# One gate block earlier beside the read-back of y, and a two-part order for two input blocks of layer 1

## The chip, the cores and the metric

The kernel runs on one core of one Trainium2 chip. The time is that of the device in microseconds (us); of several runs the median is given. PE is the matrix engine, DVE the vector engine, ACT the activation engine, POOL the general engine, and SP the queue that issues nearly all DMAs.

## What is computed

One inference step of a two-layer (`DEPTH = 2`) hybrid backbone over 1152 tokens, 128 of context and 1024 latent, with 1024 channels. Cut to what matters:

```python
h = rmsnorm(x, norm_g) * (1.0 + scale) + shift
a_in, a_gate, f_in, f_gate, q, k, v, c_gate = jnp.split(h @ w_in, SPLITS, axis=-1)
ya, finals = s5_mixer(a_in, ...)                    # the state-space branch; its result is "y"
za = jax.nn.gelu(ya) @ glu_w
ya = za[..., :BRANCH_W] * jax.nn.sigmoid(za[..., BRANCH_W:])
yf = fourier_mix(f_in) @ fnet_w
yc = blocked_attention(rope(q), rope(k) + context, v + context)
proj = [branch_n * silu(gate_n) @ w_branch[n] for n in (a, f, c)]
g = jax.nn.sigmoid(h @ merge_w + merge_b)           # three gates of 1024 channels
out = x + gate * (sum(g[n] * proj[n]) @ w_out)
```

## The kernel before

**Dense blocks.** Nearly all PE work is in dense blocks: 128 output channels for the 1152 tokens. The tokens are three chunks (j = 0, 1, 2) of 384. A value is held as a rounded high part and a low part, and each product is three matmuls (high x high, low x high, high x low): a block over 1024 channels is 3 x 8 x 3 = 72 matmuls of 128x384, one over 512 channels is 36. Results go to a PSUM tile `pd`, of which there are two; ACT or DVE empties it ("evicts") before the next but one chunk can start. Weights are loaded by SP into `wst` (512 rows at a time), split by ACT (`whi`) and POOL (`wlo`) one unit ahead; a chunk's inputs are `hh`/`hl` for h, and the tile `A1` (rows show it as A) for a branch's values read back from DRAM.

**A list and its driver.** `layer` fills a list of blocks in a fixed order with `dense_add`, and `dense(n)` takes the next n from it. It yields after each 4 input groups, so a gate block has 6 steps of 12 matmuls and a block over 512 channels has 3. `drive`, `beside` and `run_some` mix these steps with other work. The framework's scheduler then orders each engine's instructions by its own forecast, so that work may move ahead of the place where it was written. Every engine runs its instructions in that order and waits at the first that can't run.

**Stages that matter here, in each layer.** (1) Input blocks: `a_in` first (`store_blocks`, 4 blocks), while the last chunk of h is still being normalised at the start of layer 1 (`h_gen(l + 1, xT, acc, (2,))`). (2) Scan and output of the state-space branch, which ends with y in DRAM. (3) The "u" stage: y is read back and split (`zload_landed`: 12 loads `yl`, then a number of bare yields, then 12 splits on ACT and DVE into A1), beside gate blocks; then 8 Glu blocks, with the modulation sums of `ada_side_gen` (`aacc`, DVE) beside them. (4) The "f" stage: the Fourier branch, beside 4 gate blocks. (5) The "a" stage: attention. It is 64 steps (8 heads x 8 groups of 128 queries). A step is: 6 matmuls of scores (`pa`), their maximum on DVE (`at_mx`), exp on ACT (`at_P`), scaling on DVE, 9 transposes on PE, their split on ACT and DVE (`at_PT`); every second step ends with 18 matmuls (`pv`). There is one `pa`, so the next scores wait for the exp. Each step hands one dense step to PE: `run_some(m, k)`. Over the stage attention yields room for 78 dense steps, and `merges` holds 18 + 6 + 24 + 6 + 24 = 78. (6) The "c" stage: the attention's result is read back and split (`zload_gen(zc_d, ...)`), beside gate blocks whose results `thc` live in a pool that opens when attention's pool closes.

Of the kernel before, what the change touches and what calls it, by code (L numbers as in the profile page):

```python
# [11 lines left out]
AF = mybir.ActivationFunctionType  # L12
# [19 lines left out]
C_AIN, C_AG, C_FIN, C_FG, C_Q, C_KV, C_CG = 0, 512, 1024, 1536, 2048, 2560, 2816  # L32
# [70 lines left out]
class Program:  # L103
# [1186 lines left out]
    def zload_landed(self, z_d, zf, tag):  # L1290
        ts = []
        for j in range(3):
            for b in range(4):
                t = self.sb(tag, [128, 384], bufs=12, pool=self.gp)
                self.dma_rows(z_d, b, j, t, False)
                ts.append((j, b, t))
        for _ in range(3):
            yield 1
        for i, (j, b, t) in enumerate(ts):
            s = slice(384 * j, 384 * j + 384)  # L1300
            self.act(zf[:, 0, b, s], t)
            self.tt(zf[:, 1, b, s], t, zf[:, 0, b, s].bitcast(F), OP.subtract)
            if i % 4 == 3:
                yield 1
# [29 lines left out]
    def layer(self, l, cs):  # L1334
        nc, I = self.nc, self.I
        w_in = I["w_in"][l]
        dt_ = lambda n, shape, ty=F: self.dp.tile(list(shape), ty, name=f"{n}{l}")
        f_d, za_d, zb_d, zc_d = (dt_(n, (512, NT)) for n in ("fd", "zad", "zbd", "zcd"))
        a_d, y_d = ((dt_(n + "p", (512, SP)), dt_(n + "l", (512, SL))) for n in ("ad", "yd"))
# [10 lines left out]
        zt = {}  # L1350

        def rows(d, b, j):
            return d[128 * b:128 * b + 128, 384 * j:384 * j + 384]

        def th_tile(tag="th", bufs=3):
            return self.sb(tag, [128, 384], bufs=bufs, pool=self.gp)

        def glu_blocks():
            out = []
            for b in range(4):  # L1360
                th = {}
                def evb(j, ps, th=th):
                    th[j] = th_tile()
                    self.act(th[j], ps, AF.Tanh, scale=0.5)
                def eva(j, ps, b=b, th=th):
                    sg = self.jt(rows(sg_d[0], b, j))
                    o = self.jo()
                    self.stt(o, th.pop(j), 1.0, ps, OP.add, OP.mult)
                    self.stt(o, o, 0.5, sg, OP.mult, OP.mult)
                    self.dma(rows(za_d, b, j), o)  # L1370
                r = zrhs(lambda: zt["y"])
                out.append(dict(w=self.colblk(I["glu_w"][l], 512, b, 4), nk=4, rhs=r, evac=evb))
                out.append(dict(w=self.colblk(I["glu_w"][l], 0, b, 4), nk=4, rhs=r, evac=eva))
            return out
# [15 lines left out]
        def gate_block(n, b, th):  # L1390
            def ev(j, ps):
                t = self.jo() if "d" in th else th_tile("thc", 24) if n == 2 else th_tile()
                self.act(t, ps, AF.Tanh, bias=self.hmb[l][:, 8 * n + b:8 * n + b + 1], scale=0.5)
                if "d" in th:
                    self.dma(rows(th["d"], b, j), t)
                else:
                    th[j] = t
            return dict(w=self.colblk(I["merge_w"][l], 1024 * n, b), nk=8, rhs=self.rhs_h, evac=ev)
# [22 lines left out]
        thb = {"d": dt_("thb", (D, NT))}  # L1421
# [30 lines left out]
                                rhs=lambda k, j: (self.mh[j][:, k], self.ml[j][:, k]), evac=ev))  # L1452
            return out

        self.dense_add(self.store_blocks(w_in, C_AIN, 4, a_d, AF.Copy))
        self.dense_add(self.store_blocks(w_in, C_FIN, 4, f_d, AF.Copy))
        self.dense_add(self.store_blocks(w_in, C_AG, 4, sg_d[0], AF.Silu))
        self.dense_add(self.store_blocks(w_in, C_FG, 4, sg_d[1], AF.Silu))
        self.dense_add(self.store_blocks(w_in, C_CG, 4, sg_d[2], AF.Silu))
        self.dense_add([gate_block(0, b, tha) for b in range(8)])  # L1460
        self.dense_add([gate_block(1, 0, thb)])
        self.dense_add(glu_blocks())
        self.dense_add([gate_block(1, b, thb) for b in range(1, 6)])
        self.dense_add(fw_blocks())
        self.dense_add([gate_block(1, 6, thb)])
        self.dense_add([proj_block(0, b, tha, "a") for b in range(8)])
# [7 lines left out]
        run = self.run_all  # L1474
        with self.spool:
            with self.epool:
                if l == 0:
                    with self.pool("gp", l, "s"):
                        drive((self.dense(4), 40), (self.ssm_setup_gen(l), 2))
                else:  # L1480
                    run(self.dense(4))
                if l == 0:
                    for k in range(KD):
                        self.dma(self.xT_d[0][128 * k:128 * k + 128, :], self.xT0[:, k])
                with self.pool("gp", l, "m"):
                    drive((self.dense(4), 47), (self.state_gen(l, a_d), 29))
            with self.pool("qp", l):
                with self.pool("gp", l, "q"):
                    self.qkt = self.qkv_tables(l)
                    def qkv():  # L1490
                        yield from self.qkv_gen(l, qs_d, k_d, v_d, (0,))
                        yield from self.qkv_gen(l, qs_d, k_d, v_d, (1,))
                    q = qkv()
                    self.run_some(q, 8)
                    drive((self.scan_gen(l), 103), (self.dense(12), 140))
                    drive((q, 78), (self.dense(2), 21))
                    self.finals(l)
                with self.pool("gp", l, "o"):
                    drive((self.dense(6), 12*6), (self.ssm_out_gen(l, a_d, y_d), 33), (self.qtail_gen(), QT))
        with self.pool("gp", l, "u"):  # L1500
            zt["y"] = self.sb("A1", [128, 2, 4, NT], R)
            run(self.beside(self.zload_landed(y_d, zt["y"], "yl"), self.dense(1), 1))
            drive((self.dense(8), 47), (self.ada_side_gen(l, self.gp, (4, 5)), 6))
        with self.pool("gp", l, "f"):
            self.fnet_tables()
# [2 lines left out]
            drive((self.dense(3), 48), (self.fnet_gen(l, f_d, zt["f"]), 48))  # L1508
        with self.pool("gp", l, "a"):
            def merges():  # L1510
                yield from self.dense(5)
                zt["a"] = self.sb("A1", [128, 2, 4, NT], R)
                yield from self.beside(self.zload_gen(za_d, zt["a"], False, HELD), self.dense(1), NA)
                yield from self.dense(8)
                zt["b"] = self.sb("A1", [128, 2, 4, NT], R)
                yield from self.beside(self.zload_gen(zb_d, zt["b"], False, 2), self.dense(1), 1)
                yield from self.dense(8)
            m = merges()
            for k in self.attn_gen(l, qs_d, k_d, v_d, sg_d[2], zc_d):
                self.run_some(m, k)  # L1520
            run(m)
# [65 lines left out]
    def run(self):  # L1587
        self.open_ssm(0)
        with ExitStack() as cs:
            self.np_ = cs.enter_context(self.tc.tile_pool(name="np", bufs=1))  # L1590
            self.xp = cs.enter_context(self.tc.tile_pool(name="xp", bufs=1))
            self.setup()
            self.xT0 = xT = self.sb("A1", [128, KD, NT])
            ssq = self.sb("ssqt", [128, 2, 9], pool=self.xp)
            self.rb = {}
            self.xr0 = self.sb("xr0", [128, KD, 384], pool=self.xp)
            ada = self.ada_first_gen(0, self.xp, (2, 0, 3, 1))
            xg = self.x_gen(xT, ssq)
            self.run_some(xg, 6)
            self.h_tiles((0,))  # L1600
            self.rb_first(ssq, 0)
            for k in range(KD):
                self.xr_first(xT, k)
            next(ada)
            self.run_some(xg, 2)
            next(ada)
            self.run_some(xg, 4)
            self.h_tiles((1,))
            self.rb_first(ssq, 1)
            for k in range(4):  # L1610
                self.h_first(xT, 0, k)
            next(ada)
            for k in range(2):
                self.h_first(xT, 1, k)
            next(ada)
            with self.tc.high_priority():
                for k in range(4, 8):
                    self.h_first(xT, 0, k)
            self.run_all(ada)
            for k in range(2, 5):  # L1620
                self.h_first(xT, 1, k)
            self.run_all(xg)
            self.h_tiles((2,))
            self.rb_first(ssq, 2)
            for k in range(5, 8):
                self.h_first(xT, 1, k)
            for k in range(KD):
                self.h_first(xT, 2, k)
        for l in range(DEPTH):
            for j in range(3):  # L1630
                self.debug(f"hh{l}", self.hh[j].bitcast(F), (slice(None), slice(None), slice(384 * j, 384 * j + 384)))
            with ExitStack() as cs:
                xT, acc = self.layer(l, cs)
                if l + 1 < DEPTH:
                    self.run_all(self.h_gen(l + 1, xT, acc, (2,)))
                else:
                    self.run_all(self.final_gen(xT, acc, (2,)))
# [25 lines left out]
```

## Time and profile before

| what | us |
|---|---|
| median of 3 runs | 2710.02 (2704.8 to 2712.21) |
| the profiled execution | 2707.93 |
| its span, first to last instruction | 2706.2 |
| PE busy in the span | 2599.8 |
| DVE, ACT, POOL busy | 1746.8, 1200.5, 655.4 |

The times are of the whole launch; the span leaves out 1.7 us around the first and the last instruction. The start of a matmul in the trace is measured and its end modelled, so a full stream of 128x384 matmuls shows rows that overlap.

### The profile page before, as it was taken

To read this page: it belongs to the slowest core of one execution; us is meant where nothing else is said; L and a number is where in the kernel's file an instruction comes from. 1 tells how busy PE (TensorE), PEld (TensorE's weight loads), DVE (VectorE), ACT (ScalarE), POOL (GpSimd) and SP (SyncE) were. 2 spreads that over 40 slices of the span, in tenths; PEclk is the share of its full clock that TensorE was granted. 3 is DMA by queue.
4 is the path that set the end of the run, shared out by engine and by line. 5 is a ranking of instruction groups with operands and counts; after the bars stand their busy time and mean duration, and the time that the engine had idled before them with its cause. 6 is when DMAs were issued, how large, how long until landed. Compare 5 with 4: busy or idle time off the path is not lost. (4 is left out here: it accounts for less than half of the span.)

```text
span 2706.2 us, 44496 instructions
## 1 busy us (share of the span) xinstructions
PE 2599.8 (96%) x16093; PEld 2502.1 (92%) x16093; DVE 1746.8 (65%) x3837; ACT 1200.5 (44%) x2754; POOL 655.4 (24%) x518
## 2 busy tenths in 40 slices
PE   6999999999999999999999999989999999999998
PEld 4999999899999899999989999989999998999997
DVE  6559964636478889847462798564654788981443
ACT  5462245741355465423345322575224556543244
POOL 1332122312321020132333312232222212101223
PEclk8999999999999999999999999999999999999999
DMA  7533233566443435535542322345645334442334
GB/s 258 154 103 102 90 105 106 168 185 199 149 139 110 143 118 154 188 96 138 172 134 86 112 86 83 119 131 166 210 142 192 104 116 155 148 125 80 92 117 145
DMA packets 459812, 366.85 MB, mean 136 GB/s; under 512 B 72816, under 2 KB 431816, under 8 KB 459592
## 3 DMA queue, kind: packets, MB, share of 16 engines
q1 hardware_dynamic: 458168, 359.68, 43.4%
q0 software_dynamic: 1424, 4.33, 0.5%
q8 instruction: 127, 2.08, 0.3%
q14 instruction: 93, 0.76, 0.1%
HBM read 243.52 MB, written 120.39 MB: 134 GB/s over the span
## 5 line engine op out<-in xcount | busy, mean ns | idle before, releaser
L169 PE MATMUL pd<-hh,whi 128*128 128x384 f32 x2496 | 854.3, 343 | 8.8 <-ACT jo L143 4.5
L169 PE MATMUL pd<-hh,wlo 128*128 128x384 f32 x2496 | 842.9, 338 | 4.7 <-POOL wlo L146 4.4
L169 PE MATMUL pd<-hl,whi 128*128 128x384 f32 x2496 | 840.2, 337 | 0.8 <-DVE hl L150 0.8
L146 POOL TENSOR_TENSOR wlo<-wst,whi 128x512 fp32r<-128x512 f32 x312 | 432.8, 1389 | 1523.1 <-ACT whi L143 1445.4
L169 PEld LDWEIGHTS pd<-hh,whi 128*128 128x128 f32 x2496 | 470.9, 189 | 14.9 <-ACT jo L143 6.1
L169 PEld LDWEIGHTS pd<-hh,wlo 128*128 128x128 f32 x2496 | 470.8, 189 | 10.0 <-POOL wlo L146 9.0
L169 PEld LDWEIGHTS pd<-hl,whi 128*128 128x128 f32 x2496 | 471.3, 189 | 2.9 <-DVE hl L150 1.9
L169 PE MATMUL pd<-A,whi 128*128 128x384 f32 x1728 | 457.7, 341 | 6.3 <-ACT jo L143 6.3
L143 ACT ACTIVATE whi<-wst 128x512 fp32r<-128x512 f32 x312 | 195.6, 630 | 291.1 <-PE pd L169 188.2
L169 PEld LDWEIGHTS pd<-A,whi 128*128 128x128 f32 x1728 | 310.9, 189 | 9.0 <-ACT jo L143 6.9
L169 PE MATMUL pd<-A,wlo 128*128 128x384 f32 x864 | 293.5, 340 | 0.0
L1107 DVE TENSOR_REDUCE at_mx<-pa 128x1 f32<-128x1152 f32 x128 | 173.2, 1353 | 16.0 <-PE pa L169 15.6
L143 ACT ACTIVATE at_PT<-pt 128x384 fp32r<-128x384 f32 (+1 forms) x260 | 114.9, 490 | 142.6 <-PE pt L174 142.2
L169 PE MATMUL pa<-at_K,at_Q 128*128 128x384 f32 x768 | 167.1, 347 | 7.8 <-ACT at_P L143 5.3
L143 ACT ACTIVATE at_P<-pa,at_mx 128x1152 f32<-128x1152 f32 x128 | 158.0, 1235 | 20.6 <-DVE at_mx L1107 19.4
L169 PEld LDWEIGHTS pd<-A,wlo 128*128 128x128 f32 x864 | 163.2, 189 | 0.1
L169 PEld LDWEIGHTS pa<-at_K,at_Q 128*128 128x128 f32 x768 | 128.2, 188 | 28.2 <-ACT at_P L143 25.2
L169 PE MATMUL pt<-qkW,hh 128*128 128x384 f32 x576 | 151.9, 345 | 0.5 <-DVE qk_xn L146 0.5
L169 PE MATMUL pv<-at_PT,at_V 128*128 128x256 f32 x1152 | 148.8, 283 | 0.0
L143 ACT ACTIVATE jo<-pd 128x384 f32<-128x384 f32 x120 | 58.1, 485 | 199.9 <-PE pd L169 113.0
L169 PEld LDWEIGHTS pv<-at_PT,at_V 128*128 128x128 f32 x1152 | 144.7, 191 | 0.8
L146 DVE TENSOR_TENSOR at_PT<-pt,at_PT 128x384 fp32r<-128x384 f32 (+1 forms) x260 | 133.1, 550 | 9.3 <-ACT at_PT L143 8.6
(297 smaller groups left out, 3719.5 us busy)
## 6 DMA issues: line engine op xcount, KB each, us to landing
aw<-in_ada_w_dram SPq DMA_DIRECT2D x48, 512.0 KB, 4.5
wst<-in_merge_w_dram SPq DMA_DIRECT2D x96, 256.0 KB, 2.9
wst<-in_w_in_dram SPq DMA_DIRECT2D x80, 256.0 KB, 3.0
td<-jo SPq DMA_DIRECT2D x96, 192.0 KB, 1.9
jt<-td SPq DMA_DIRECT2D x96, 192.0 KB, 2.7
wst<-in_w_out_dram SPq DMA_DIRECT2D x64, 256.0 KB, 2.8
sgd<-jo SPq DMA_DIRECT2D x72, 192.0 KB, 1.8
jt<-sgd SPq DMA_DIRECT2D x64, 192.0 KB, 3.0
```

The lines of the kernel that those rows point to most:

```text
L143: return self.nc.scalar.activation(out, in_, func, **kw)
L146: return (e or self.nc.vector).tensor_tensor(out=out, in0=a, in1=b, op=op)
L169: return self.nc.tensor.matmul(out, w, x, start=first, stop=last, **kw)
L1107: nc.vector.tensor_reduce(out=mx[:, 0:1], in_=src, axis=AX.XY if m3 else AX.X, op=OP.max, negate=True)
```

## The change

In the u stage of both layers two gate blocks stand beside the read-back of y instead of one, and the splits start after five bare yields instead of three. The second gate block comes out of the attention stage, whose `merges` starts with `dense(4)` instead of `dense(5)`: the Fourier stage still takes four gate blocks, each one further on in the list. Attention then has room for 78 dense steps, and `merges` holds 72. In layer 1 alone, the first two of the four `a_in` blocks are cut in two parts: chunks 0 and 1 of both, then chunk 2 of both. Each part loads and splits its weights, so four weight units more are loaded, and `dense(6)` covers the same twelve chunks as `dense(4)` did.

```diff
--- before.py
+++ after.py
@@ -1294,7 +1294,7 @@
                 t = self.sb(tag, [128, 384], bufs=12, pool=self.gp)
                 self.dma_rows(z_d, b, j, t, False)
                 ts.append((j, b, t))
-        for _ in range(3):
+        for _ in range(5):
             yield 1
         for i, (j, b, t) in enumerate(ts):
             s = slice(384 * j, 384 * j + 384)
@@ -1452,15 +1452,18 @@
                                 rhs=lambda k, j: (self.mh[j][:, k], self.ml[j][:, k]), evac=ev))
             return out
 
-        self.dense_add(self.store_blocks(w_in, C_AIN, 4, a_d, AF.Copy))
+        ain = self.store_blocks(w_in, C_AIN, 4, a_d, AF.Copy)
+        if l > 0:
+            ain = [dict(ain[b], js=js) for js in ((0, 1), (2,)) for b in (0, 1)] + ain[2:]
+        self.dense_add(ain)
         self.dense_add(self.store_blocks(w_in, C_FIN, 4, f_d, AF.Copy))
         self.dense_add(self.store_blocks(w_in, C_AG, 4, sg_d[0], AF.Silu))
         self.dense_add(self.store_blocks(w_in, C_FG, 4, sg_d[1], AF.Silu))
         self.dense_add(self.store_blocks(w_in, C_CG, 4, sg_d[2], AF.Silu))
         self.dense_add([gate_block(0, b, tha) for b in range(8)])
-        self.dense_add([gate_block(1, 0, thb)])
+        self.dense_add([gate_block(1, b, thb) for b in (0, 1)])
         self.dense_add(glu_blocks())
-        self.dense_add([gate_block(1, b, thb) for b in range(1, 6)])
+        self.dense_add([gate_block(1, b, thb) for b in range(2, 6)])
         self.dense_add(fw_blocks())
         self.dense_add([gate_block(1, 6, thb)])
         self.dense_add([proj_block(0, b, tha, "a") for b in range(8)])
@@ -1478,7 +1481,7 @@
                     with self.pool("gp", l, "s"):
                         drive((self.dense(4), 40), (self.ssm_setup_gen(l), 2))
                 else:
-                    run(self.dense(4))
+                    run(self.dense(6))
                 if l == 0:
                     for k in range(KD):
                         self.dma(self.xT_d[0][128 * k:128 * k + 128, :], self.xT0[:, k])
@@ -1499,7 +1502,7 @@
                     drive((self.dense(6), 12*6), (self.ssm_out_gen(l, a_d, y_d), 33), (self.qtail_gen(), QT))
         with self.pool("gp", l, "u"):
             zt["y"] = self.sb("A1", [128, 2, 4, NT], R)
-            run(self.beside(self.zload_landed(y_d, zt["y"], "yl"), self.dense(1), 1))
+            run(self.beside(self.zload_landed(y_d, zt["y"], "yl"), self.dense(2), 1))
             drive((self.dense(8), 47), (self.ada_side_gen(l, self.gp, (4, 5)), 6))
         with self.pool("gp", l, "f"):
             self.fnet_tables()
@@ -1508,7 +1511,7 @@
             drive((self.dense(3), 48), (self.fnet_gen(l, f_d, zt["f"]), 48))
         with self.pool("gp", l, "a"):
             def merges():
-                yield from self.dense(5)
+                yield from self.dense(4)
                 zt["a"] = self.sb("A1", [128, 2, 4, NT], R)
                 yield from self.beside(self.zload_gen(za_d, zt["a"], False, HELD), self.dense(1), NA)
                 yield from self.dense(8)
```

The first place is ACT's order in the u stage of layer 0: `jo<-pd` is the eviction of a gate chunk, `A_6450<-yl` a split of y, `th<-pd` the eviction of a Glu chunk. Before:

```order
L143 ACTIVATE A_6450<-yl 128x384 x3
L143 ACTIVATE whi<-wst 128x512
L143 ACTIVATE A_6450<-yl 128x384 x3
L143 ACTIVATE jo<-pd,hmb_115 128x384
L143 ACTIVATE A_6450<-yl 128x384 x2
L143 ACTIVATE th<-pd 128x384 x2
```

With the change:

```order
L143 ACTIVATE A_6450<-yl 128x384 x3
L143 ACTIVATE whi<-wst 128x512
L143 ACTIVATE jo<-pd,hmb_115 128x384
L143 ACTIVATE A_6450<-yl 128x384 x5
L143 ACTIVATE jo<-pd,hmb_115 128x384 x2
L143 ACTIVATE whi<-wst 128x512 x2
L143 ACTIVATE jo<-pd,hmb_115 128x384
L143 ACTIVATE th<-pd 128x384 x2
```

The eviction of the first gate block's third chunk now stands ahead of the last five splits, and the three evictions of the second gate block stand between the splits and the Glu evictions. On PE the second block's 72 matmuls stand ahead of the first Glu matmul.

The second place is PE's order where attention ends in layer 0: `pa` are scores, `pt`/`pv<-ident` transposes, `pv<-at_PT` the products with V, and `pd` dense matmuls. Before, from the last dense matmuls ahead of the last products:

```order
L169 MATMUL pd<-hh_303,whi 128x384
L169 MATMUL pv<-at_PT_12364,at_V 128x256 x9
L169 MATMUL pv<-at_PT_12365,at_V 128x256 x9
L169 MATMUL pd<-hl_304,whi 128x384
L169 MATMUL pd<-hh_303,wlo 128x384
L169 MATMUL pd<-hh_303,whi 128x384
```

With the change, from the scores of the last step:

```order
L169 MATMUL pa<-at_K,at_Q 128x384
L169 MATMUL pv<-at_PT_12320,at_V 128x256 x9
L169 MATMUL pv<-at_PT_12321,at_V 128x256 x9
L169 MATMUL pa<-at_K,at_Q 128x384 x5
L174 MATMUL pt<-ident,at_P 128x128 x6
L174 MATMUL pv<-ident,at_P 128x128 x3
L174 MATMUL pt<-ident,at_P 128x128 x6
L174 MATMUL pv<-ident,at_P 128x128 x3
L169 MATMUL pv<-at_PT_12406,at_V 128x256 x9
L169 MATMUL pv<-at_PT_12407,at_V 128x256 x9
L169 MATMUL pd<-hh_472,whi 128x384
```

Before, 10 dense matmuls stand between the last transposes and the last products, and 23 of a chunk that is already begun follow them. With the change no dense matmul stands in the last three steps, and the first behind them begins the third chunk of a gate block, whose PSUM tile must first be emptied. The two chunks ahead of it (48 matmuls) were drawn into the steps 57 to 61.

The third place is PE's order at the start of layer 1, from the transposes (`rs`) that start chunk 2 of h: `hh_14830`, `hh_15097` and `hh_15204` are chunks 0, 1 and 2. Before:

```order
L174 MATMUL pt<-ident,rs 128x128 x3
L169 MATMUL pd<-hh_15097,whi 128x384
L169 MATMUL pd<-hl_15098,whi 128x384
L169 MATMUL pd<-hh_15097,wlo 128x384
L169 MATMUL pd<-hh_15204,whi 128x384
```

With the change:

```order
L174 MATMUL pt<-ident,rs 128x128 x3
L169 MATMUL pd<-hh_14830,whi 128x384
L169 MATMUL pd<-hl_14831,whi 128x384
L169 MATMUL pd<-hh_14830,wlo 128x384
L169 MATMUL pd<-hh_14830,whi 128x384
```

Before, 3 matmuls stand between these transposes and the first that needs chunk 2; with the change 39 do (15 on chunk 0 and 24 on chunk 1 of the second block).

## Rows read from the trace of the kernel before

**Rows 1.** The page: span, then busy time, share and instructions of each engine.
```profile
span 2706.2 us, 44496 instructions
PE 2599.8 (96%) x16093; PEld 2502.1 (92%) x16093; DVE 1746.8 (65%) x3837; ACT 1200.5 (44%) x2754; POOL 655.4 (24%) x518
```

**Rows 2.** Waits of PE over the span: total us, times, longest us.
```profile
PE pd L169 <- ACT jo L143: 10.8, 7, 3.2
PE pt L174 <- DVE at_P L1111: 8.1, 12, 1.0
```

**Rows 3.** Timeline, layer 0's y stage: start, us, engine, operation, [idle before <-releaser].
```profile
591.15 0.34 PE L169 MATMUL pd<-A,wlo 128*128 128x384 f32 x1
593.15 1.01 ACT L143 ACTIVATE A<-yl 128x384 fp32r<-128x384 f32 x2 [0.93 <-DMA yl<-ydl]
594.07 0.56 ACT L143 ACTIVATE jo<-pd,hmb 128x384 f32<-128x384 f32 x1
594.69 1.01 PE L169 MATMUL pd<-A,whi 128*128 128x384 f32 x2 [3.20 <-ACT jo L143]
600.50 0.52 PE L169 MATMUL pd<-A,whi 128*128 128x384 f32 x2
```

**Rows 4.** Windows after the y wait, both layers: busy us, PEclk.
```profile
595.00:600.00 5.00, 5.00 (x17) 5.00 (x17) 3.97 (x8) 1.33 (x4) 0.00 (x0) 0.50 0.93 294
1916.00:1918.00 2.00, 2.00 (x12) 2.00 (x13) 1.18 (x3) 1.11 (x3) 0.00 (x0) 1.00 0.92 297
```

**Rows 5.** Timeline of PE, layer 1's y stage.
```profile
1915.96 0.62 PE L169 MATMUL pd<-A,whi 128*128 128x384 f32 x2 [3.10 <-ACT jo L143]
1916.59 0.51 PE L169 MATMUL pd<-A,whi 128*128 128x384 f32 x2
1920.75 0.51 PE L169 MATMUL pd<-A,whi 128*128 128x384 f32 x2
```

**Rows 6.** Timeline of PE, first input blocks of layer 1.
```profile
1389.16 0.45 PE L169 MATMUL pd<-hl,whi 128*128 128x384 f32 x1 [0.26 <-DVE hl L150]
1390.16 0.54 PE L174 MATMUL pt<-ident,rs 128*128 128x128 f32 x3 [0.38 <-POOL rs L146]
1392.59 1.01 PE L169 MATMUL pd<-hh,whi 128*128 128x384 f32 x2 [1.36 <-ACT hh L143]
1395.31 0.48 PE L169 MATMUL pd<-hh,whi 128*128 128x384 f32 x1
```

**Rows 7.** Timeline of DVE, first gated products of layer 0.
```profile
603.89 0.55 DVE L150 SCALAR_TENSOR_TENSOR jo<-th,pd 128x384 f32<-128x384 f32 x1 [3.21 <-issue]
604.36 0.74 DVE L150 SCALAR_TENSOR_TENSOR aacc<-aw,silc,aacc 128x512 f32<-128x512 f32 x1
```

**Rows 8.** Timeline, last attention steps of layer 0 and the first eviction after them.
```profile
1098.48 0.81 DVE L1111 TENSOR_SCALAR at_P<-at_P,at_mx 128x1152 f32<-128x1152 f32 x1
1104.66 1.22 PE L169 MATMUL pa<-at_K,at_Q 128*128 128x384 f32 x6
1105.91 1.36 DVE L1107 TENSOR_REDUCE at_mx<-pa 128x1 f32<-128x1152 f32 x1 [0.16 <-PE pa L169]
1107.37 1.24 ACT L143 ACTIVATE at_P<-pa,at_mx 128x1152 f32<-128x1152 f32 x1
1108.72 0.16 DVE L1110 RECIPROCAL at_mx<-at_mx 128x1 f32<-128x1 f32 x1
1111.34 0.84 PE L174 MATMUL pt<-ident,at_P 128*128 128x128 f32 x6 [0.98 <-DVE at_P L1111]
1114.11 2.31 PE L169 MATMUL pv<-at_PT,at_V 128*128 128x256 f32 x18
1118.94 0.58 ACT L143 ACTIVATE thc<-pd,hmb 128x384 f32<-128x384 f32 x1 [1.14 <-DVE jo L146]
```

**Rows 9.** Timeline of PE, attention steps with waits in the middle of layer 0.
```profile
943.48 1.31 PE L169 MATMUL pa<-at_K,at_Q 128*128 128x384 f32 x6 [1.28 <-ACT at_P L143]
948.76 1.31 PE L169 MATMUL pa<-at_K,at_Q 128*128 128x384 f32 x6
```

## Prediction

> **What bounds the kernel.** The page comes first. PE is busy 2599.8 of 2706.2 us, so 106 us are left, and no other engine comes near it [rows 1]. The reader should take from this that the kernel is PE's instruction stream, and that a change of order can win or lose only by what PE stands idle, or by a clock that falls. The change takes no product away, so I count idle time, place by place.
>
> The second view is the list of PE's waits. Its largest entry is `pd` waiting for an eviction on ACT, 10.8 us in 7 waits, the longest 3.2; next are transposes waiting for the scaling on DVE, 8.1 us in 12 short waits [rows 2]. So one wait is long, and attention has many small ones.
>
> The third view is the timeline around the long wait. In layer 0 PE stops after 591.15 and starts again at 594.69; the eviction that it waits for starts at 594.07, directly behind a split of y which had waited for its DMA [rows 3]. ACT is in order, so a gate chunk's eviction was caught behind splits whose data was not there. Layer 1 repeats it with 3.10 us [rows 5].
>
> One scale for all sums: 24 matmuls start between 1916.59 and 1920.75 [rows 5], so a dense matmul is 0.173 us, a dense step of 12 is 2.08, a gate block 12.5. Anything under 0.3% (8.1 us) is about what a measurement of this kernel can't tell from no change.
>
> **The u stage: gain.** The order of the changed program puts the eviction ahead of the last five splits, and 12.5 us of matmuls ahead of the first Glu matmul. The late splits are nearly through at 594.07 in layer 0 [rows 3]; the Glu block's second chunk, where the wait stood at 591, comes at about 604 now. The wait goes. In layer 0 it is worth 3.2 us, and a second sum: after it 17 matmuls stand in the 5 us from 595 to 600, with the granted clock at 0.50, the lower of the two levels (1.2 GHz) [rows 4]. Between 594.69 and 600.50 [rows 3] 18 start in 5.8 us instead of 3.1, which is 2.7 lost. In layer 1 the wait is 3.1 us and the clock stays at 1.00 [rows 4, 5]. Gain 5.9 + 3.1 = 9.0.
>
> A rule speaks for a larger price than the second row: the Trainium skill (TensorE: Matmul & The Clock Gate, "HAM oscillation") says that idle gaps of PE put it back to the slow clock and are paid a second time. By it both gaps would cost 5.9. The trace agrees in layer 0 and not in layer 1.
>
> **The u stage: what is moved in.** The second block brings its weights (two loads, already one unit ahead of PE), three evictions, and three stores on SP, ahead of loads for the modulation sums. Those sums now all but fill DVE before the first gated product: by the order 22 of their instructions stand there instead of 6. Sixteen more at 0.74 are 11.8 us. DVE had 3.21 us idle before that product [rows 7], and PE comes to it later by 12.5 less the wait that went (6.6 in layer 0, 9.4 in layer 1). So DVE is late by 2 us in layer 0 and not in layer 1, and the second `pd` hides 2.08 of it. I take 0.5 a layer, 1.0 in all; the bounds are 0, and 4 if the sums' loads, now behind stores on SP, come late as well.
>
> **Layer 1's first blocks: gain.** PE waits 0.26 for the low part of chunk 1, 0.38 for the transposes' input, and 1.36 for chunk 2; after the last, 8 matmuls take from 1392.59 to 1395.31, 1.3 longer than at full clock [rows 6]. Sum 3.3. With 39 matmuls (6.8 us) between the transposes and chunk 2, nearly all of that has cover. The four extra weight units cost ACT and POOL a little over 2 and 5 us in a stretch where neither binds; I price them at nothing, with 2 us as the upper bound if a split comes late. So 3.3, bounds 1 and 5.
>
> **Attention: what is taken out.** The moved block's 6 steps were PE's filling in attention: 78 steps were there for 78 places, and 72 are now. Attention starts no earlier, because the scheduler lets Glu's successors, the `fnet_w` blocks, run ahead of it as far as the gate block did; so the steps are missing at the end. What an unfilled step costs can be read from the last ones of before [rows 8]. Scores start at 1104.66, their maximum at 1105.91 (1.36), the exp at 1107.37 (1.24) to 1108.61; the next scores need that. Chain 4.1 us. PE's own work in a step is 6 scores and 9 transposes, 2.0; every second step has 18 products (2.3).
> - Step 62, nothing beside it: 4.1 - 2.0 = **2.1** idle.
> - Step 61: the products stand between the scores, which lengthens the chain by 2.3, and a split of the attention's result, drawn forward, takes 0.5 on ACT ahead of the exp [a split: rows 3]: 6.9. PE has 2.0 + 2.3 + 7 dense (1.2) = 5.5. **1.4**.
> - Step 63: chain to the end of the exp 4.0 + 2.3 + 0.5, then the reciprocal (starts 0.1 later, 0.16), one drawn-forward split on DVE (0.5), the scaling (0.81) and 0.1: 8.5. PE has 4.3. **4.2**.
> - Last transposes to last products: 1111.34 to 1114.11 is 2.8 and had 10 dense matmuls in it; 1.0 is the transposes' own. **1.8**.
> - End of the products (1116.42) to the end of the first eviction after attention (1119.52): before, 23 matmuls lay over it; now the next PE instruction needs the tile that it empties. **3.1**.
> - Steps 59 and 60 have 12 dense matmuls each, so chain and PE are level; drawn-forward splits cost 0.2 or 0.3 each: **0.5**.
>
> Sum 13.1; the 0.98 us that PE already waited there [rows 8] goes off: 12.1 a layer. Layer 1 has the same order, so 24.2. That chains of this length are real is seen where attention waits already: two scores start 5.28 us apart from 943.48 to 948.76, the first after 1.28 us idle [rows 9].
>
> Of the two long waits before, one cost 2.7 us more in clock and one nothing; the end of attention ends in a 3.1 us wait after a stretch that is half idle. I take half of 2.7 a layer: 2.7 in all. Bounds for attention's loss: 7 a layer (the chain without drawn-forward splits, partly overlapped), 17 (clock low over the last two steps as well).
>
> **Sum.** 24.2 + 2.7 - 9.0 - 3.3 + 1.0 = 15.6 us longer. The profiled execution took 2707.93, so 2723.5; the median of the runs lies 2.1 above that execution. I say 2724, 0.5% slower.
>
> **Rivals.**
> *A. The end of attention costs little more than its last wait* (same). The scheduler had spread 48 matmuls of later gates over steps 57 to 61, and if PE is late against the chain by then, the unfilled steps partly catch up. Then a layer loses some 5 us, 10 in all, against 11.3 gained: 2709. For it: before, PE hardly waits in these steps, so DVE and ACT may run with slack that shows nowhere. Against it: the last four terms are chains of single instructions with no slack to use.
> *B. Attention gets shorter by what is taken out of it* (faster). Mechanism: in attention DVE and ACT set the pace and PE's filling only lengthens steps; fewer fillings, shorter steps, and no price. Place: steps 57 to 64. It decides once attention's loss is under 1.6 us a layer (11.3 - 8.1 = 3.2 for both). Time: 2710 - 11.3 = 2699. For it: the 12 waits on scaling [rows 2] show a chain near PE's pace with filling. Against it: those waits are 1.0 us at most and the last eviction's 3.1 has no cover left.
> *C. The clock falls in each unfilled end* (slower still). Half speed on the last two steps' products lengthens the chain by 2.3 in steps 61 and 63, and 2.7 follow as in layer 0: up to 7 a layer in place of the 1.35 taken, 2735. No row shows a half-idle stretch of that length. The rule of the Trainium skill (TensorE: Matmul & The Clock Gate, "HAM oscillation") points this way.
> *D. The y wait stays*, since the splits still stand ahead of evictions on ACT. Then 9.0 goes off the gains: 2733. Against it: the eviction that was caught is now ahead of the late splits.
>
> **Chances.** Forecast 0.60, its own range 2716 to 2732; A 0.18; B 0.12; C and D 0.10. Faster by over 0.3%: B, 0.12. Within 0.3%: A and the lowest edge of the forecast, 0.20. Slower by over 0.3%: 0.68. The range takes in A and part of C and D: 2706 to 2734.
>
> **What would show it.** Right: no wait of 3 us on ACT's eviction near 594 and 1916; PE's waits at the end of both attention stages of 2, 4, 2 and 3 us, the last one for ACT's `thc`; no 1.36 us wait for `hh` at the start of layer 1; some 24 us more idle in the two ends. Wrong: if the scores of steps 61 to 63 start under 4 us apart, if the last eviction waits for nothing and comes at once, or if PE waits over 2 us for gated products on DVE in the Glu blocks.

## The result: 1.3% slower, and the profile after

The changed kernel takes 2745.64 us (median of 4 runs, 2743.01 to 2750.24), the kernel before 2710.02 beside it: ratio 1.0132, 95% interval 1.012 to 1.0144, some 36 us. The forecast was 2724 with a range to 2734. The direction is right, the size is not. PE does the same matmuls; what changed is how long it stands idle and at which clock it runs.

The page of the changed kernel, first lines, to be held against [rows 1]: as many matmuls, 12 us more of busy time (a slower clock makes them longer), 38 us more span.
```profile
span 2743.8 us, 44537 instructions
PE 2612.1 (95%) x16093; PEld 2514.0 (92%) x16093; DVE 1753.2 (64%) x3837; ACT 1204.6 (44%) x2758; POOL 657.0 (24%) x522
```
The waits of PE in the changed kernel (total, times, longest), against [rows 2]. The second line is new, two waits in all; the first has two more waits and a longest of 3.8 instead of 1.0.
```profile
PE pt L174 <- DVE at_P L1111: 15.3, 14, 3.8
PE pd L169 <- DVE jo L150: 10.9, 2, 6.3
...
PE pd L169 <- ACT thc L143: 4.5, 2, 2.2
```
**The Glu stage.** Timeline of the changed kernel, PE and DVE, both layers. In front of the first gated product (`jo<-th,pd`), which empties a `pd` tile, stand 22 instructions of the modulation sums. PE has two `pd` tiles, fills both, and stops.
```profile
598.87 0.88 DVE L365 TENSOR_SCALAR aacc<-aw,silc 128x512 f32<-128x512 f32 x2 [4.04 <-DMA aw<-in_ada_w_dram]
599.67 11.43 DVE L150 SCALAR_TENSOR_TENSOR aacc<-aw,silc,aacc 128x512 f32<-128x512 f32 x14
...
611.08 0.34 PE L169 MATMUL pd<-A,wlo 128*128 128x384 f32 x1
615.39 0.54 DVE L150 SCALAR_TENSOR_TENSOR jo<-th,pd 128x384 f32<-128x384 f32 x1
615.99 1.01 PE L169 MATMUL pd<-A,whi 128*128 128x384 f32 x2 [4.57 <-DVE jo L150]
...
1933.90 1.57 DVE L365 TENSOR_SCALAR aacc<-aw,silc 128x512 f32<-128x512 f32 x2 [5.42 <-DMA aw<-in_ada_w_dram]
1951.11 0.54 DVE L150 SCALAR_TENSOR_TENSOR jo<-th,pd 128x384 f32<-128x384 f32 x1
1951.70 1.01 PE L169 MATMUL pd<-A,whi 128*128 128x384 f32 x2 [6.35 <-DVE jo L150]
```
**The end of attention, layer 0.** Timeline of PE in the changed kernel, to be held against [rows 8]. Five waits, 10.2 us (10.4 in layer 1); the 18 products at 1127.03 take 4.21 us, those of step 61 took 2.30.
```profile
1111.41 1.33 PE L169 MATMUL pa<-at_K,at_Q 128*128 128x384 f32 x6 [1.08 <-ACT at_P L143]
1115.75 0.44 PE L169 MATMUL pa<-at_K,at_Q 128*128 128x384 f32 x1 [1.89 <-ACT at_P L143]
1116.03 2.30 PE L169 MATMUL pv<-at_PT,at_V 128*128 128x256 f32 x18
...
1123.99 1.22 PE L174 MATMUL pt<-ident,at_P 128*128 128x128 f32 x6 [3.81 <-DVE at_P L1111]
...
1127.03 4.21 PE L169 MATMUL pv<-at_PT,at_V 128*128 128x256 f32 x18 [1.17 <-DVE at_PT L146]
1133.47 0.44 PE L169 MATMUL pd<-hh,whi 128*128 128x384 f32 x1 [2.24 <-ACT thc L143]
```
Windows of the changed kernel behind these waits: Glu stage of both layers, then the ends of attention. A row has the window and its length, then busy us and count of instructions of PE, its weight loads, DVE, ACT and POOL, then PEclk (the granted clock as a share of the upper level), the DMAs' share and GB/s. At full clock 5 us hold 28.9 dense matmuls of 0.173 us.
```profile
616.00:621.00 5.00, 5.00 (x20) 5.00 (x21) 5.00 (x9) 0.63 (x1) 0.60 (x1) 0.69 0.72 229
1952.00:1957.00 5.00, 5.00 (x17) 5.00 (x17) 4.69 (x9) 0.63 (x1) 0.62 (x1) 0.50 0.75 236
...
1125.00:1130.00 5.00, 3.83 (x19) 3.43 (x18) 1.67 (x3) 1.08 (x3) 0.00 (x0) 0.50 0.28 86
1133.00:1138.00 5.00, 4.53 (x17) 4.53 (x18) 0.87 (x2) 2.35 (x5) 0.68 (x1) 0.66 0.84 265
2474.00:2479.00 5.00, 5.00 (x17) 5.00 (x17) 0.99 (x2) 1.38 (x3) 0.80 (x1) 0.50 0.60 175
```
**The start of attention, layer 0.** Timeline of the changed kernel, ACT and PE. Splits of the Glu result (`A<-jt`, read back from `zad`) stand on ACT with their loads not landed; behind them wait attention's own copies, and PE.
```profile
771.58 0.53 ACT L143 ACTIVATE A<-jt 128x384 fp32r<-128x384 f32 x1 [1.29 <-DMA jt<-zad]
774.16 0.52 ACT L143 ACTIVATE A<-jt 128x384 fp32r<-128x384 f32 x1 [1.18 <-DMA jt<-zad]
...
775.71 0.70 PE L169 MATMUL pv<-at_PT,at_Vp 128*128 128x512 f32 x2 [1.68 <-DVE at_Yp L146]
778.60 1.32 PE L169 MATMUL pa<-at_K,at_Q 128*128 128x384 f32 x6 [1.48 <-ACT at_P L143]
```
**Layer 1's start.** Timeline of PE in the changed kernel, against [rows 6]: the wait for chunk 2 (`hh`) falls from 1.36 to 0.57, and one of 1.99 for the low part of a weight (`wlo`) comes in; before, the longest of that kind here was 0.38, at 1400.38.
```profile
1414.76 0.44 PE L169 MATMUL pd<-hh,whi 128*128 128x384 f32 x1 [0.57 <-ACT hh L143]
...
1425.15 0.45 PE L169 MATMUL pd<-hh,wlo 128*128 128x384 f32 x1 [1.99 <-POOL wlo L146]
```
**The first gate block of the Fourier stage.** Timeline of PE in the changed kernel, both layers. These two waits were 1.66 and 1.50 before; behind them PEclk is 0.66 over 5 us (19 and 21 matmuls), before it was 1.00.
```profile
672.61 0.45 PE L169 MATMUL pd<-hh,whi 128*128 128x384 f32 x1 [2.10 <-ACT jo L143]
2010.83 0.45 PE L169 MATMUL pd<-hh,whi 128*128 128x384 f32 x1 [3.53 <-ACT jo L143]
```

### The profile page after: what moved, and what is told of

Its sections match the earlier page's. It is cut to its first block, busy times and chain, and to the rows that moved or that the text cites. A ratio compares the mean times of both kernels' runs of the same rounds, so it can differ in the third digit from the quotient of the medians.

```text
span 2743.8 us, 44537 instructions
## 1 busy us (share of the span) xinstructions
PE 2612.1 (95%) x16093; PEld 2514.0 (92%) x16093; DVE 1753.2 (64%) x3837; ACT 1204.6 (44%) x2758; POOL 657.0 (24%) x522
## 3 DMA queue, kind: packets, MB, share of 16 engines
q8 instruction: 127, 2.08, 0.3%
## 5 line engine op out<-in xcount | busy, mean ns | idle before, releaser
L146 POOL TENSOR_TENSOR wlo<-wst,whi 128x512 fp32r<-128x512 f32 x316 | 435.9, 1381 | 1559.5 <-ACT whi L143 1462.5
L169 PEld LDWEIGHTS pd<-A,whi 128*128 128x128 f32 x1728 | 311.1, 190 | 13.0 <-DVE jo L150 11.6
```

What stands on the lines that cost most here:

```text
L146: return (e or self.nc.vector).tensor_tensor(out=out, in0=a, in1=b, op=op)
L169: return self.nc.tensor.matmul(out, w, x, start=first, stop=last, **kw)
```

## The experiments

The theory is that attention's unfilled ends and the Glu products behind the sums cost separately, and that beneath them the change gains what was forecast. There are three rivals: the u stage itself disturbs attention; the late products cost nothing that would not be waited for elsewhere; the block's gain never existed. Differences in us are the ratio to the kernel before, measured on the same chip, times 2710.

**e1: the chunks alone.** The kernel before with the change's two hunks on layer 1.
```
+        if l > 0:
+            ain = [dict(ain[b], js=js) for js in ((0, 1), (2,)) for b in (0, 1)] + ain[2:]
...
-                    run(self.dense(4))
+                    run(self.dense(6))
```

> Only the chunk order of layer 1 is changed; the Glu stage, the Fourier stage and attention are those of before. Theory (the chunk order gains what PE waited for chunk 2, and the losses all lie in the other part): the 1.36 us wait for hh at the start of layer 1 goes, 3 us are gained, 2707 (2704 to 2709). Rival (the wait only moves to the low part of a weight or a split, as the 2.15 us wait seen in the changed kernel hints): 2710, within 1.5 us of before.

2705.66 us, ratio 0.9989 (0.9978 to 1.0001): 3 us faster, 0 to 6. The median is where the theory has it, but no change at all isn't excluded. The wait for `wlo` (1.98 us) is there as well: POOL has four more splits. The traces speak for less than 3: from PE's wait for DVE's `ssq` at 1380.50 (kernel before) to PE's wait for `jo` at 1518.08 stand 792 matmuls, and the same stretch takes 136.2 to 137.7 us in the five kernels without the chunk order (mean 137.1) and 135.0 to 138.2 in the seven with it (mean 136.7).

**e5: attention's block alone.** The kernel before, the block moved to the Fourier stage.
```
-            drive((self.dense(3), 48), (self.fnet_gen(l, f_d, zt["f"]), 48))
+            drive((self.dense(4), 48), (self.fnet_gen(l, f_d, zt["f"]), 48))
...
-                yield from self.dense(5)
+                yield from self.dense(4)
```


> The kernel before, but one gate block is taken from attention and put beside the Fourier stage's work (four blocks there instead of three); the u stage and layer 1's chunks are untouched. Theory (72 steps for 78 places cost 14 to 16 us at each end of attention): 24 to 30 us slower than before, less what the Fourier stage gains from more cover: 2728 to 2740. Rival (the unfilled ends cost little by themselves, and the loss comes from the u stage): less than 10 us slower, 2710 to 2720.

2744.69 us, 1.0124 (1.0105 to 1.0143): 34 us slower, more than either had. With no change in the u stage the same five waits stand at both ends, and the two waits at attention's start as well. Timeline of PE in this kernel: one wait at the start, the longest at each end.
```profile
773.80 0.71 PE L169 MATMUL pv<-at_PT,at_Vp 128*128 128x512 f32 x2 [1.61 <-DVE at_Yp L146]
1122.75 1.51 PE L174 MATMUL pt<-ident,at_P 128*128 128x128 f32 x6 [3.81 <-DVE at_P L1111]
2463.89 1.51 PE L174 MATMUL pt<-ident,at_P 128*128 128x128 f32 x6 [3.78 <-DVE at_P L1111]
```
So the u stage isn't what disturbs attention.

**e8: the read-back alone.** The kernel before, all 78 steps, but gate block 5 behind the Fourier product instead of ahead of it, so that the read-back of the Glu result starts one block earlier.
```
-        self.dense_add([gate_block(1, b, thb) for b in range(1, 6)])
+        self.dense_add([gate_block(1, b, thb) for b in range(1, 5)])
...
-        self.dense_add([gate_block(1, 6, thb)])
+        self.dense_add([gate_block(1, b, thb) for b in (5, 6)])
...
-                yield from self.dense(5)
+                yield from self.dense(4)
...
-                yield from self.dense(8)
+                yield from self.dense(9)
```


> The kernel before with all 78 steps in attention, but two of its blocks change places, so that the read-back of the Glu result and its splits start one block (12.5 us) earlier in attention. Theory (the two waits of 1.7 and 1.5 us at the start of attention in the changed kernel are ACT standing at splits whose loads are not there, and need only the earlier read-back): those waits appear with attention filled to its end, 3 to 7 us slower than before, 2713 to 2718. Rival (they come from the missing block): no such wait, within 2 us of before.

2712.45 us, 1.0018 (1.0006 to 1.0029): 5 us slower, 2 to 8. Timeline of PE in this kernel: the two waits are there with attention filled to its end. So they belong to the earlier read-back.
```profile
762.53 0.70 PE L169 MATMUL pv<-at_PT,at_Vp 128*128 128x512 f32 x2 [1.71 <-DVE at_Yp L146]
765.55 2.29 PE L169 MATMUL pa<-at_K,at_Q 128*128 128x384 f32 x6 [1.61 <-ACT at_P L143]
```

**e9: useless work in the gaps.** The kernel of e5 (its edit isn't shown again), and the last two `w_branch` blocks of the second branch compute each chunk twice.
```
+                for r in range(b.get("rep", 0)):
+                    self.dense_ahead(u0)
+                    hi, lo = self.usplit[u0]
+                    for k in range(nk):
+                        self.mm3(ps[:, :w], (hi[:, k % 4], lo[:, k % 4]), b["rhs"](k, j), k == 0, k == nk - 1)
+                    yield 4 * 3 * 163
...
+        self.dense_add([dict(proj_block(1, b, thb, "b"), rep=b // 6) for b in range(8)])
```


> The kernel before with one gate block taken from attention (which alone was 34 us slower), but its last two projection blocks compute each chunk twice, the second pass writing over the first, so that 72 repeated matmuls (12.5 us a layer) stand where the block was missing. Theory (an unfilled step costs the wait and the fall of the clock after it, together more than the filling itself): the waits of 1 to 4 us at both ends go, PEclk stays at 1.00 there, and useless work makes the kernel faster, by 2 to 5 us a layer: 25 to 30 us slower than before, 2735 to 2740. Rival (the unfilled ends cost their waits of 10.2 us a layer alone, and the rest of the 34 us lies elsewhere): the repeats cost 2.3 us a layer more than the waits, 2748 to 2750.

2740.25 us, 1.0117 (1.0102 to 1.0131): 32 us slower than before, 2 less than e5 though PE does 25 us more. The long waits at the ends are gone, those at attention's start stay. Windows of this kernel at attention's end: the clock stays at 1.00.
```profile
1120.00:1125.00 5.00, 4.01 (x27) 3.72 (x26) 4.94 (x10) 2.32 (x5) 1.29 (x1) 1.00 0.04 13
1125.00:1130.00 5.00, 5.00 (x38) 4.99 (x36) 1.96 (x5) 1.74 (x5) 0.00 (x0) 1.00 0.83 262
```
So the unfilled ends cost about what 12.5 us of filling a layer costs, and perhaps a little more: 25 + 2 = 27 us in all by e9, 34 - 5 = 29 by e5 and e8. The 2 us between e9 and e5 are within their intervals. Waits without a clock price would have put e9 4.6 us above e5, which is at the edge of what these intervals allow; that the clock has a price at the ends is read from the rows (18 products in 4.21 us instead of 2.30).

**e2: the block given back.** The changed kernel with one block moved from the Fourier stage to attention.
```
-            drive((self.dense(3), 48), (self.fnet_gen(l, f_d, zt["f"]), 48))
+            drive((self.dense(2), 48), (self.fnet_gen(l, f_d, zt["f"]), 48))
...
-                yield from self.dense(4)
+                yield from self.dense(5)
```

> The changed kernel, but the gate block that attention lost is given back to it (its merges take five blocks first, as before), and the Fourier stage has one block less beside its work. Theory (attention's loss is the missing filling): the gaps of 1.3 to 4 us at the end of both attention stages go, some 30 us of the changed kernel's time come back, less what the Fourier stage loses for want of cover (0 to 6 us a layer): 2716 to 2728. Rival (attention's end suffers from what the u stage does to order and clock, not from the missing block): the gaps stay, 2740 or more.

2713.68 us, 1.0016 (1.0005 to 1.0026): 4 us slower than before, 31 faster than the changed kernel. None of the new waits is left at attention's ends or start; each end has one of 0.99, as before (0.98). The time lies below the forecast's 2716: the Fourier stage lost less than feared. The two waits for gated products stay: 11.5 us, the longer 6.2.

**e3: products ahead of sums.** The changed kernel; on DVE the sums from the third unit on are queued behind the first Glu block's products.
```
+            with self.tc.issue_after(self.prod[min(i - 2, 2)].ins) if behind and i > 1 else ExitStack():
+                for h in range(2):
...
-            drive((self.dense(8), 47), (self.ada_side_gen(l, self.gp, (4, 5)), 6))
+            g, self.prod = self.dense(8), []
+            self.run_some(g, 6)
+            drive((g, 35), (self.ada_side_gen(l, self.gp, (4, 5), behind=True), 6))
```


> The changed kernel, but on DVE the modulation sums from the third unit on are put behind the gated products of the first Glu block (8 sums stand ahead of the first product, not 22 instructions). Theory (PE's waits of 4.57 and 6.35 us in the Glu stage are the sums that stand ahead of products): both waits go, and the clock's fall with them, 11 to 17 us faster than the changed kernel: 2729 to 2735. Rival (DVE is simply late there, with its loads, so that the same wait comes a block later, or the transfer of the sums' weights sets the time): within 4 us of the changed kernel, 2742 to 2749.

2727.38 us, 1.0067 (1.0053 to 1.0081): 18 us of the 36 come back, a little more than the 11 to 17 expected, and both waits for gated products are gone. DVE's timeline in this kernel: eight sums, then the product, which DVE now waits for.
```profile
596.77 6.26 DVE L150 SCALAR_TENSOR_TENSOR aacc<-aw,silc,aacc 128x512 f32<-128x512 f32 x6
606.99 0.56 DVE L150 SCALAR_TENSOR_TENSOR jo<-th,pd 128x384 f32<-128x384 f32 x1 [3.96 <-issue]
```

**e10: the sums' loads ahead of stores.** The changed kernel; SP issues two of the sums' loads right behind y's, and the sums take them up (cut here).
```
...
+        self.pre = {k: self.ada_load(self.ul, self.gp, 3, 4, k) for k in range(2)}
         for _ in range(5):
             yield 1
```


> The changed kernel, but SP issues the first two weight loads of the modulation sums right behind y's twelve loads, ahead of the three stores of gate chunks. On DVE 23 instructions stand ahead of the first gated product instead of 22. Theory (of PE's waits of 4.57 and 6.35 us some 3 and 4 us are the sums' loads standing behind stores on SP, the rest is the sums' own length): the sums start 3 to 4 us earlier, the waits shrink to 1 to 3 us, and 6 to 12 us of the changed kernel's time come back: 2733 to 2740. Rival (only the number of sums ahead of the product counts, since the third load or DVE's speed holds them anyway): the waits stay within 1 us, 2743 to 2748.

2739.65 us, 1.0107 (1.009 to 1.0124): about 7 us back, 1 to 12. The two waits for products are 1.8 and 2.1 us, from 4.57 and 6.35, with PEclk 1.00 behind them. Not all of that fall is loads that stood behind stores on SP. Counted from y's first load, the sums start 3.9 and 4.9 us earlier than in the changed kernel, DVE then waits 2.3 and 2.6 for their third load, and the product comes 1.8 and 3.2 earlier. The last 1.0 in each layer is PE, which comes later, behind new waits of 0.65 and 0.80 for `jo` on ACT.
```profile
596.01 0.88 DVE L365 TENSOR_SCALAR aacc<-aw,silc 128x512 f32<-128x512 f32 x2 [1.08 <-DMA aw<-in_ada_w_dram]
596.81 4.06 DVE L150 SCALAR_TENSOR_TENSOR aacc<-aw,silc,aacc 128x512 f32<-128x512 f32 x6
```

**e7: three steps ahead of y's splits.** e3, and in `zload_landed`:
```
-        for _ in range(5):
+        for _ in range(3):
```

> The changed kernel with the products' order mended, but three gate steps ahead of the splits of y instead of five, as before. Theory (the eviction of a gate chunk is caught behind splits whose data is not there, and the five steps are what frees it): a wait of some 3 us on ACT's eviction is back in both layers, 6 to 9 us slower than with five steps, 2733 to 2737. Rival (the second block of matmuls alone covers y's way, wherever the splits stand): within 2 us of 2727.

2732.72 us, 1.0081 (1.0063 to 1.0099). Neither forecast fits whole: the eviction wait is back, but as 1.1 and 0.9 us, not 3, and the time's interval overlaps e3's. The second block covers most of y's way by itself; what the five steps add to that is some 2 us of waits.

**e4: five steps, one block.** The kernel before, and in `zload_landed`:
```
-        for _ in range(3):
+        for _ in range(5):
...
-            if i % 4 == 3:
+            if i == 3:
```

> The kernel before, with its one gate block in the u stage, but five of its six steps ahead of the splits of y, then four splits, the last step and the other eight. Theory (the order frees the evictions, but one block is too short for y's way): the wait of 3 us on ACT's eviction goes, and PE waits about as long for the splits at the first Glu matmul, 2708 to 2712, no change. Rival (the eviction's order alone was the loss): up to 9 us faster, 2701 to 2706.

2708.4 us, 0.9995 (0.9986 to 1.0005): no change. The order alone gains nothing that can be told. The trace isn't quite the theory's: the wait for `jo` on ACT is gone in layer 0 and 1.1 us in layer 1, PE does not wait for the splits, and shorter waits, of up to 0.9 us each for gated products, come in. They sum to 1.8 and 3.5 us, from 3.2 and 3.1.

**e6: both losses undone.** The diffs of e2 and e3 together.

> The changed kernel with both losses undone: attention has its block back (one block less beside the Fourier stage), and on DVE the sums from the third unit on stand behind the first gated products. Theory (the two losses are separate and add, and the change's own gains are there beneath them): 2713.7 less the 18 us that the products' order brought alone, some 2696 (2692 to 2701), faster than before by 0.3% or more. Rival (the block in the u stage gains nothing: the y wait's 9 us come back as waits further on, in the Fourier stage): 2704 or more, no faster than with the chunk order alone.

2697.91 us, 0.9963 (0.995 to 0.9976): 10 us faster than before, 46 faster than the changed kernel. It beats both, and shows that the u stage's gain was real: some 7 us beyond e1, with one block less beside the Fourier stage. The traces show where: from y's first load on SP to attention's first scores, with the same matmuls, 168.3 us before and 162.1 here in layer 0 (lines below), 166.4 and 160.9 in layer 1; in e1 the stretches are 167.8 and 166.1.
```profile
581.74 0.33 SPq L128 DMA_DIRECT2D yl<-ydp  x1
750.00 1.20 PE L169 MATMUL pa<-at_K,at_Q 128*128 128x384 f32 x6
...
580.91 0.33 SPq L128 DMA_DIRECT2D yl<-ydp  x1
743.05 1.20 PE L169 MATMUL pa<-at_K,at_Q 128*128 128x384 f32 x6
```
The first two lines are of the kernel before. That queueing the sums behind the products would gain something without the second block was not run; the list of PE's waits of the kernel before has none for gated products.

## Why the prediction failed in size, step by step

| term | forecast, us | runs |
|---|---|---|
| attention's ends: waits and clock | +24.2 and +2.7 | +27 (e9) to +29 (e5 less e8); rows: 18.6 and 8.8 |
| read-back of the Glu result, one block earlier | none | +5 (e8) |
| products behind sums | +1.0 | +14.5 (rows), 18 (e3) |
| u stage: y wait and clock | -9.0 | -9 (what is left), -7 beside a thinner Fourier stage (e6) |
| layer 1's chunks | -3.3 | -3, 0 to -6 (e1); the traces speak for less |

What is left for the u stage's gain: 36 - 34 (e5) + 3 (e1) = 5, less the 14.5 of the line above it. So the -9 is no measurement; only e6 shows that gain by itself, and in size only roughly: 7 us in time beyond e1, 11.6 in the stretches of its one trace. One loss has no line: the first gate block of the Fourier stage, which stands some 2.5 us longer in waits than before and loses (28.9 - 19) x 0.173 + (28.9 - 21) x 0.173 = 3.1 in clock. The prediction had nothing for it. These waits go from 0.9 to 3.7 us in the other kernels, so how much of it belongs to the change is open; if all of it does, the u stage gained that much more than 9.

The forecast's own sum, 15.6, added to the median before would have been 2725.6; it says 2724. That changes nothing below: 36 us were measured.

**The step that failed is "The u stage: what is moved in".** It priced the sums ahead of the gated products at 0.5 us a layer, 1.0 in all, with 4 as the upper bound; they cost 14.5 by the rows and 18 by e3. PE waited 4.57 and 6.35 us, and the clock behind the waits took (28.9 - 20) x 0.173 = 1.5 and (28.9 - 17) x 0.173 = 2.1 more. Of the step's parts, PE's delay was right (in layer 0 the first chunk was ready at 609.3, 28.4 behind y's first load at 580.92 on SP; before it was 22.1; so 6.3, forecast 6.6; in layer 1 it is 9.5, forecast 9.4). Three others were not:
- The loads. From y's first load to the first sum 17.95 us pass in layer 0 and 18.65 in layer 1; before it was 15.14 and 14.27. That is 2.8 and 4.4 late. On SP three stores and a weight load stand between y's loads and the sums' now, two stores before; the first of the sums' loads is issued 2.0 and 2.4 later, and the rest is a longer way to landing. The prediction named this and bounded it at 4 for both layers together; it is 7.2, and in e10 the products come 5.0 earlier.
- The slack. The 3.21 us of [rows 7] is layer 0's alone. In the kernel before, layer 1's timeline of DVE has none: the last sums end at 1923.29, where the product begins, 0.8 after its chunk was ready. The row of one layer was used for both.
```profile
1920.84 2.45 DVE L150 SCALAR_TENSOR_TENSOR aacc<-aw,silc,aacc 128x512 f32<-128x512 f32 x2 [0.45 <-DMA aw<-in_ada_w_dram]
1923.21 0.54 DVE L150 SCALAR_TENSOR_TENSOR jo<-th,pd 128x384 f32<-128x384 f32 x1
```
- The length. Sixteen more instructions took 12.7 us (598.87 to 615.39 less the 3.8 that the first six took before), not 11.8: a transpose and a reduction of 1.2 each, and sums that took longer beside POOL.

Layer 0: 2.8 + 12.7 - 3.2 - 6.3 = 6.0 late; less the 2.08 of a second `pd`, and with the product itself (0.54), that is about the 4.57 seen. Layer 1: 4.4 + 12.1 (its sixteen) + 0.8 - 9.5 = 7.8 late, and by the same sum about the 6.35 seen. The test at the end of the prediction (over 2 us of waits for gated products) is what came true.

**Attention.** The sum of this step, 26.9, was nearly right, its parts were not; that the two errors nearly cancel is luck. The five waits of the list (forecast 2.1, 1.4, 4.2, 1.8 and 3.1; measured 1.89, 1.08, 3.81, 1.17 and 2.24) are each a little shorter, 20.6 for both layers, and 18.6 without the 0.98 that each had before. The clock's share is over three times the 2.7 taken: rival C in part. In layer 0 it is 4.21 - 2.30 = 1.9 on the last products and 4.53 - 17 x 0.173 = 1.6 behind the last wait; in layer 1 it is 1.9 and 2.1, and 3.61 - 2.30 = 1.3 on the products before (timeline of PE in the changed kernel):
```profile
2454.99 3.61 PE L169 MATMUL pv<-at_PT,at_V 128*128 128x256 f32 x18
```
What no step saw is that merges which start one block sooner start their read-back one block sooner too, so that splits stand on ACT before their loads have landed: the same kind of wait that the change removes from y. It cost the 5 us of e8.

**The y wait** went, as forecast, and rival D fell. But the times of e7 and e4 put it down to the second block's 12.5 us; the five steps add little. Rivals A and B fell with e5.

**Layer 1's start** came out as forecast by e1's median, but its interval reaches no change, and cover for chunk 2 isn't what gained: the wait for `hh` fell by 0.8, while 2 us went to `wlo`, the bound that the prediction named, so that PE's waits there sum to 3.1 us in e1 and 2.7 before. What is in e1's favour is the clock: PEclk of two 5 us windows there (from 1381 and 1391) is 1.00, 0.66 before. The first of them lies ahead of anything that the change of order moves, so part of that is chance.

## What to carry to other kernels

When filling is moved, look at who stands in line at the place that it leaves and at the place that it enters, on every in-order queue: here SP's loads behind stores and DVE's products behind side work, at either end of one block. Side work with its own deadline far away should be queued behind the products that PE waits for, not ahead. A slack that is read in one layer has to be read in the other too. And where a term of an account is what is left over from the total, it can hide a loss that nobody looked for, as at the Fourier stage's first block here.

## What the hardware showed beside

**A sum waits for POOL.** In e3 six sums took 6.26 us while two `wlo` splits of POOL (597.12 and 599.20) lay over them; the same six took 4.06 in e10, where POOL was idle until 601.54. That is 1.1 us for each. The Trainium skill (SBUF — State Buffer, "SBUF: two separate sides") says that a VectorE instruction with two SBUF operands and a GpSimd instruction that reads SBUF hold one pair of ports as a lock, so that the later one stands still. The rows agree for these two operations: the 1.1 us are most of a split's 1.3. Nothing in the prediction's price of 0.74 a sum allowed for it.

**The clock after a wait.** Behind waits of 1.8 and 2.1 us (e10) PEclk was 1.00, behind 4.57 it was 0.69 over 5 us and behind 6.35 it was 0.50; before the change 3.20 had 0.50 and 3.10 had 1.00 [rows 3 to 5]. At attention's end it fell to 0.50 behind waits none of which was over 3.81, with PE busy 12.0 of the 20 us from 1110 to 1130. And in the changed kernel it fell behind a single wait of 2.10: PEclk is 0.63 from 673 to 676. So the length of a wait alone does not tell here: 3.20 and 2.10 were followed by the lower level (1.2 GHz), 3.10 and 2.12 were not.

The rule that was weighed (TensorE: Matmul & The Clock Gate, "HAM oscillation", of the Trainium skill) has idle gaps put PE back to the slow clock. The rows agree at 4.57 and 6.35, and disagree with it as the prediction applied it, to every gap.
